# A scan with chunked steps in a hybrid inference kernel: outputs once per step, one diagonal for both heads' inverse, values token-major through DRAM, low-rank products in row halves

## The chip, the cores and the metric

One Trainium2 chip, and of it one core. The metric is device time in microseconds (us) of one execution. In profiles the engines are PE (TensorE's products), PEld (its weight loads), DVE (VectorE), ACT (ScalarE), POOL (GpSimd) and SP (SyncE, whose queue issues every DMA of this kernel, in order).

## What is computed

One step of a two-layer network on 1,024 latent tokens and 256 context tokens of width 1,024. Layer 0 is a dense projection, a bidirectional RWKV-7 scan over 8 heads of 64, a short convolution, and an output projection; layer 1 is attention. The change touches the scan of layer 0 only:

```python
def rwkv_scan(S0, r, w, k, v, kk, a, reverse):
    def step(S, inp):
        r_t, w_t, k_t, v_t, kk_t, a_t = inp
        sk = jnp.einsum('bhvk,bhk->bhv', S, kk_t)
        S = (S * w_t[:, :, None, :] - sk[..., None] * (kk_t * a_t)[:, :, None, :]
             + v_t[..., None] * k_t[:, :, None, :])
        return S, jnp.einsum('bhvk,bhk->bhv', S, r_t)
...
    w_log = -jax.nn.softplus(-(w0 + jnp.einsum('bldr,drc->bldc', jnp.tanh(lw), lw2))) - 0.5
    decay = jnp.exp(-jnp.exp(w_log.astype(f32)))
    a = jax.nn.sigmoid(a0 + jnp.einsum('bldr,drc->bldc', la, la2))
```

The scan runs forwards and backwards, both outputs are added, normalised per head, and gated.

## The kernel before

**The fill.** Layer 0's dense projection is 816 triples of products (`mm<-h_hi,whi`, `mm<-h_lo,whi`, `mm<-h_hi,wlo`: float32 split into two reduced-precision parts), 2,448 matmuls in `dense_g`. Its results are shifted and stored to DRAM in `rkv_d` (keys, normalised keys, r, v), `lora_d` and `sg_d` by the sinks of `s_part` and `a_part`.

**The scan.** Heads go in four pairs; a pair fills 128 partitions, 64 per head. A pair has five steps: four groups of 256 latent tokens, where step j does group j forwards and group 3-j backwards, and one step for the context. So there are 20 steps, each with two directions d and four chunks i of 64 tokens. A step goes through these generators:

- `load` and `prepare`: loads, the low-rank products `iv<-lor,lw` (both directions, 64 rows each, for decay and a), exponentials; makes `bk` and `s`.
- `interact`: products of keys with keys inside each chunk (`wk<-s,bk`), masked into `nn`, `br` and the other half of `s`; the transposes `wk<-ident,bk` that make `tbk`.
- `solve`: on DVE, the inverses of the 32x32 triangular diagonal blocks (`tmp`, `acc`: 62 small instructions), sent through DRAM (`w_d`) into the matrix `w`.
- `merge`: v is loaded (`vt`), transposed on PE (`iv<-ident,vt`) and copied into `hv`; then the off-diagonal block of the inverse: a transpose of one diagonal block by products with the identity (`iv<-ident,w`), a copy, products with `nn` (`iv<-t,nn`), a copy, products `iv<-w,zz`, a copy into `w`.
- `chain`: the recurrence over the four chunks, with the state in `hv`. Per chunk, in this order of dependence: `ch<-hv,s`, copy `xs`, `ch<-xs,w`, copy into `hv`, `ch<-hv,tbk`, four DVE instructions `hv<-ch,gc,hg` that write the next chunk's state. The outputs of the chunk are two groups of products, `py<-s,hv` and `py<-br,hv`, added into `y` per chunk and direction.
- `finish`: per-head normalisation (`iv<-y,ones`, `iv<-sqy,ones`), bonus, gate, store.

**What sets the order.** Each of these is a Python generator that says before each operation on which engine and for which tiles it waits. `Loom.run` is a planner with a clock per engine and a cost for each instruction: it takes the first generator in `PRECEDENCE` whose next operation could start soon enough, and issues it. So the program order on every engine is fixed when the kernel is built; on the chip, each engine runs its list in that order. The fill's generators stand low in the table, so dense triples go where no scan operation is ready. All recorded operations carry the line of one helper (L145), so the profile is read by tile names.

**Rings.** The PSUM banks are rings: `mm` 2, `wk` 2, `py` 2, `ch` 1, `iv` 1 banks. Two steps are under way at a time, by conditions such as this one, ahead of `solve`:

```python
            yield lambda: x.nr is not None and (x.n < 2 or steps[x.n - 2].done)
```

## Time and profile before

| | us |
|---|---|
| median of 3 runs (lowest to highest) | 2251.95 (2249.22 to 2253.41) |
| the profiled execution: its own time | 2253.86 |
| its span, first to last instruction | 2252.2 |
| layer 0's dense products and the scan beside them | from 64.9 to 1171.4 |
| attention layer and its projections | from there to the end |

The profiled execution is 1.9 us above the median. The last row of the scan is the product that turns the final context state round. Busy shares of the whole span are means over all stages; the stage of the scan has to be read by itself, with windows and the timeline. PE's matmuls are pipelined: the length of one overlaps the next, so the time that a group takes from PE is read from its start to the start of what follows it.

### The profile page before, as it was taken

What the parts mean: (1) busy time and instruction counts of PE and PEld (TensorE: products, weight loads), DVE (VectorE), ACT (ScalarE), POOL (GpSimd) and SP (SyncE); (2) the same over time, 40 slices, a digit from 0 to 9 for tenths busy, and PEclk for the clock granted to TensorE, in tenths of its full rate; (3) what the DMA queues carried; (4) which work ended last, traced back from release to release, by engine and by line L of the source; (5) the groups of instructions that cost most, each with busy time, mean ns of one, the idle gap of its engine ahead of it and who ended that gap; (6) DMA issues with size and microseconds to landing.
All of it is one profiled execution on the core that took longest, in us unless ns stands there. A gap on an engine that the chain in (4) does not pass through costs nothing.

```text
span 2252.2 us, 42921 instructions
## 1 busy us (share of the span) xinstructions
...
## 2 busy tenths in 40 slices
...
GB/s 271 305 98 131 98 105 131 85 68 114 102 97 103 99 96 101 85 111 54 86 153 185 206 111 88 99 87 107 82 53 48 60 42 38 43 28 71 58 131 108
DMA packets 337818, 232.86 MB, mean 103 GB/s; under 512 B 163890, under 2 KB 289860, under 8 KB 335556
## 3 DMA queue, kind: packets, MB, share of 16 engines
...
## 4 chain that ended last, share of the span: by engine, by line
PE 39%; DVE 9%; DMA 5%; issue 3%; ACT 1%; POOL 1%; SPq 1%; DVEq 0%; POOLq 0%; ACTq 0%
PE mm L145 21%; PE pv L145 8%; PE wk L145 5%; PE py L145 4%; DVE mx L145 3%; DVE rz L145 1%; DVE zs L145 1%; DMA rz<-rz_d 1%; PE ch L145 1%; DVE tmp L145 1%; SPq L145 1%; DVE acc L145 1%; DMA rz_d<-rc 1%; DMA rc<-rz 0%; DVE hv L145 0%
## 5 line engine op out<-in xcount | busy, mean ns | idle before, releaser
L145 POOL TENSOR_TENSOR zs<-zs,pe 128x512 f32<-128x512 f32 x275 | 366.8, 1370 | 34.1 <-ACT pe L145 32.1
L145 PE MATMUL mm<-h_hi,whi 128*128 128x512 f32 (+1 forms) x816 | 336.5, 412 | 4.3 <-ACT whi L145 4.1
L145 PE MATMUL mm<-h_hi,wlo 128*128 128x512 f32 (+1 forms) x816 | 299.3, 367 | 8.1 <-DVE wlo L145 7.2
L145 PE MATMUL mm<-h_lo,whi 128*128 128x512 f32 (+1 forms) x816 | 298.7, 366 | 0.0
L145 POOL TENSOR_TENSOR wlo<-wraw,whi 128x128 fp32r<-128x128 f32 x228 | 111.4, 494 | 246.0 <-ACT whi L145 205.8
L145 PE MATMUL pv<-pe,v_sb 128*64 128x512 f32 (+1 forms) x832 | 200.4, 604 | 0.0
L145 PEld LDWEIGHTS mm<-h_hi,whi 128*128 128x128 f32 x816 | 159.9, 196 | 49.5 <-issue 12.2
L145 PEld LDWEIGHTS mm<-h_hi,wlo 128*128 128x128 f32 x816 | 160.1, 196 | 37.1 <-DVE wlo L145 10.0
L145 DVE TENSOR_TENSOR acc<-acc,tmp 128x60 f32<-128x60 f32 (+23 forms) x620 | 168.0, 273 | 20.8 <-issue 2.9
L145 PE MATMUL mm<-wts,omh 128*128 128x512 f32 x648 | 166.6, 410 | 7.6 <-ACT wts L145 4.0
L145 PEld LDWEIGHTS mm<-h_lo,whi 128*128 128x128 f32 x816 | 161.0, 197 | 14.4
L145 PE MATMUL mm<-wts,h_hi 128*128 128x512 f32 x480 | 151.1, 396 | 0.0
L145 POOL TENSOR_TENSOR hg<-hv,gc 64x128 f32<-64x128 f32 x152 | 65.1, 428 | 185.0 <-DVE hv L145 173.9
L145 PEld LDWEIGHTS mm<-wts,omh 128*128 128x128 f32 x648 | 122.9, 194 | 38.0 <-ACT wts L145 5.3
L145 ACT ACTIVATE whi<-wraw 128x128 fp32r<-128x128 f32 x272 | 80.2, 305 | 78.2 <-DMA wraw<-in_w_in_e_dram 40.3
L145 DVE TENSOR_REDUCE mx<-mm 128x1 f32<-128x512 f32 (+1 forms) x138 | 89.7, 660 | 36.7 <-PE py L145 12.6
L145 DVE SCALAR_TENSOR_TENSOR hv<-ch,gc,hg 64x64 f32<-64x64 f32 x288 | 81.3, 282 | 49.3 <-PE ch L145 42.2
L145 POOL TENSOR_TENSOR xr<-xr,og 128x512 f32<-128x512 f32 x40 | 54.6, 1364 | 128.4 <-DVE og L145 93.3
L145 PEld LDWEIGHTS pv<-pe,v_sb 128*64 128x64 f32 x832 | 51.6, 139 | 93.9 <-issue 82.3
L145 DVE TENSOR_REDUCE mx<-py 128x1 f32<-128x512 f32 (+1 forms) x138 | 89.6, 660 | 28.7 <-PE mm L145 13.0
L145 DVE TENSOR_TENSOR tmp<-acc,nra 128x31 f32<-128x31 f32 (+7 forms) x320 | 90.1, 282 | 27.4 <-DMA acc<-eye_d 17.7
L145 ACT ACTIVATE pe<-py 128x512 f32<-128x512 f32 (+1 forms) x139 | 79.1, 587 | 60.3 <-PE mm L145 20.3
...
## 6 DMA issues: line engine op xcount, KB each, us to landing
...
```

Of the source, the lines that this page charges most:

```text
L145: r = f(*a, **k)
```

## The change

- **Outputs once per step.** `py` is one bank that holds both directions' 256 tokens. `chain` issues `py<-s,hv` right behind `ch<-hv,s`; a new generator `outputs` issues all `py<-br,hv` of a step at once when the four chunks are done, then one addition or copy into `y` per direction instead of one per chunk. The next chain takes the bank, so it waits for this.
- **Both heads' inverse on one diagonal.** `w` becomes 128 wide with each head's inverse in its own block, so `ch<-xs,w` is one 128-row product per direction instead of two 64-row ones. In `merge` the block's transpose is done by DVE (`STREAM_TRANSPOSE`) instead of PE and a copy; the off-diagonal block of `nn` comes from a copy in DRAM (`n12_d`, 2 stores and 2 loads per step), so `nn` needs one buffer.
- **v token-major through DRAM.** New generator `turn_v`: v is transposed right behind its dense product, forwards and backwards (PE 128x128 transposes, a reversing copy, a copy out of PSUM), and stored to `vt_d`; `values` loads `hv` from it with four DMAs per step. The transposes and copies in `merge` go. `bonus`, `merge` and `turn_v` share a ring of two tiles `t11`.
- **Low-rank products in row halves.** The two directions alternate, each into its own bank; `iv` has two banks, which also serve layer 0's first transposes in place of `py`.
- **A looser pipeline.** The conditions between steps are split: `solve` waits for its own step's inputs alone, the `tbk` transposes are a generator of their own, and flags `recurred` (the recurrence is over), `valued` and `done` (outputs too) take the place of `done`. `PRECEDENCE` has the new generators; the planner's cost for 64-row float32 products on more than 64 columns changes.

```diff
-        ((ps_mm, "mm", 2), (ps_wk, "wk", 2), (ps_py, "py", 2), (ps_ch, "ch", 1), (ps_iv, "iv", 1)))
+        ((ps_mm, "mm", 2), (ps_wk, "wk", 2), (ps_py, "py", 1), (ps_ch, "ch", 1), (ps_iv, "iv", 2)))
...
-    w_t = [rc.tile([P, 2, 4, C], F32, name=f"w{i}") for i in range(2)]
+    w_t = [rc.tile([P, 2, 4, P], F32, name=f"w{i}") for i in range(2)]
...
+    def s_v(p):
+        def sink(b, f, done):
+            t0, n, _ = BLK[b]
+            dma(out=sp[p][:, 3, t0:t0 + n], in_=f)
+            turns.append(turn_v(p, b, f, done))
+            yield lambda: True
...
+        t0, n, cd = BLK[b]
+        for z in range(2):
+            pt = None
+            for i in range(0, n, GRP):
+                x = f[:, i:i + GRP]
...
+                    back = f[:, n - i - GRP:n - i][:, ::-1]
...
+                for q in range(0, GRP, P):
+                    T.transpose(out=pt[:, i + q:i + q + P], in_=x[:, q:q + P], identity=ident)
...
+            r0 = t0 if z == 0 else NS + NT - t0 - n if cd else NS - t0 - n
+            dma(out=vt_d[p][z][r0:r0 + n].rearrange("(i q) v -> q i v", q=P),
+                in_=t[:, 0:n].rearrange("q (i v) -> q i v", v=P))
+            nbs.release(t)
...
-        for d in range(2):
-            yield "T", x.lor, lw2, iv_ps
-            pz = iv_ps.take()
-            for z in range(2):
-                T.matmul(pz[:, z * GRP:(z + 1) * GRP], lw2[HH[d], z, :], x.lor[HH[d], z, :], start=True, stop=True)
+        yield "T", x.lor, lw2, iv_ps, iv_ps
+        pzs = [iv_ps.take(), iv_ps.take()]
+        for z in range(2):
+            for d in range(2):
+                T.matmul(pzs[d][:, z * GRP:(z + 1) * GRP], lw2[HH[d], z, :], x.lor[HH[d], z, :], start=True, stop=True)
+        for d, pz in enumerate(pzs):
             for z in range(2):
...
+        for h in range(2):
+            dma(out=n12_d[x.n % 4][h], in_=x.nn.rearrange(CD)[64 * h:64 * h + 32, :, 32:64])
...
-        yield "T", w8, iv_ps
-        pa = iv_ps.take()
-        for i in range(8):
-            for h in range(2):
-                r1 = 64 * h
-                T.matmul(pa[r1:r1 + 32, i * 32:i * 32 + 32], w8[r1:r1 + 32, i, 0:32], ident[r1:r1 + 32, r1:r1 + 32],
-                         start=True, stop=True)
-        t11 = st1.tile([P, 256], F32, tag="t11", name="t11")
-        yield from copied(pa, *((t11[r:r + 32, :], pa[r:r + 32, 0:256]) for r in (0, 64)))
-        iv_ps.release(pa)
+        yield "V", w8, t11s[0]
+        t11 = t11s[0].take()
+        for rr in HH:
+            V.transpose(t11[rr].rearrange("p (i t) -> p i t", i=8), w8[rr, :, rr.start:rr.start + 32])
         yield "T", t11, iv_ps
         pa = iv_ps.take()
         for i in range(8):
             for h in range(2):
                 r1, r2 = 64 * h, 64 * h + 32
-                T.matmul(pa[r2:r2 + 32, i * 32:i * 32 + 32], bn8[r1:r1 + 32, i, 32:64], t11[r1:r1 + 32, i * 32:i * 32 + 32],
+                T.matmul(pa[r2:r2 + 32, i * 32:i * 32 + 32], x.n12[r1:r1 + 32, i, :], t11[r1:r1 + 32, i * 32:i * 32 + 32],
...
+    def values(x):
+        yield lambda: passed[f"t{x.p}"]
+        t0 = NS if x.j is None else x.j * GRP
+        for d in range(2):
+            for h in range(2):
+                dma(out=x.hv[HH[1 - h], h, d],
+                    in_=vt_d[x.p][d][t0:t0 + GRP, HH[h]].rearrange("(i t) v -> t i v", t=C))
...
+        py = x.py = py_ps.take()
         for i in range(4):
             c0 = i % 2 * 256
             pa, pu = (pc[:, c0 + q:c0 + q + 128].rearrange("p (d t) -> p d t", d=2) for q in (0, 128))
@@ -1161,13 +1216,14 @@
             for d in range(2):
                 for h, rr in enumerate(HH):
                     T.matmul(pa[rr, d], x.s[h][:, d, i, 0, :], x.hv[:, h, d, i, :], start=True, stop=True)
+            for d in range(2):
+                c1 = 256 * d + 64 * i
+                for h, rr in enumerate(HH):
+                    T.matmul(py[rr, c1:c1 + C], x.hv[:, h, d, i, :], x.s[h][:, d, i, 1, :], start=(d == 0 and i == 0),
+                             stop=False, skip_group_check=True)
             xs = chn.tile([P, 2, C], F32, tag="xs", name="xs", bufs=1)
             yield from copied(pa, (xs, pa))
-            yield "T", py_ps, py_ps
-            pys = [py_ps.take(), py_ps.take()]
-            for d in range(2):
-                for h, rr in enumerate(HH):
-                    T.matmul(pys[d][rr, 0:C], x.hv[:, h, d, i, :], x.s[h][:, d, i, 1, :], start=True, stop=False)
             if not last:
                 hg = chn.tile([P, 2, C], F32, tag="hg", name="hg", bufs=1)
                 for h, rr in enumerate(HH):
@@ -1176,8 +1232,7 @@
             yield "T", xs, x.w
             for d in range(2):
-                for rr in HH:
-                    T.matmul(pu[rr, d], x.w[rr, d, i, :], xs[rr, d], start=True, stop=True)
+                T.matmul(pu[:, d], x.w[:, d, i, :], xs[:, d], start=True, stop=True)
...
-            yield ("T",)
-            for d in range(2):
-                for h, rr in enumerate(HH):
-                    T.matmul(pys[d][rr, 0:C], x.hv[rr, h, d, i, :], x.br[rr, d, i, :], start=False, stop=True)
-            for d in range(2):
-                py = pys[d]
-                yield "V" if j is not None and j >= 2 else "S", py, 0.15
-                c0 = i * C if d == 0 else GRP - (i + 1) * C
-                ysl = y[d][:, c0:c0 + C]
-                if d == 1:
-                    ysl = ysl[:, ::-1]
-                if (j is not None and j >= 2) or c0 in seen:
-                    V.tensor_tensor(out=ysl, in0=py[:, 0:C], in1=ysl, op=ALU.add)
-                else:
-                    S.activation(ysl, py[:, 0:C], AF.Copy)
-                if j is None:
-                    seen.add(c0)
-                py_ps.release(py)
             if i < 3:
                 yield "T", x.hv[:, :, :, i + 1]
         ch_ps.release(pc)
         x.y = y
+    def outputs(x):
+        j, y, py = x.j, x.y, x.py
+        yield "T", x.hv, x.br
+        for d in range(2):
+            for i in range(4):
+                c1 = 256 * d + 64 * i
+                for h, rr in enumerate(HH):
+                    T.matmul(py[rr, c1:c1 + C], x.hv[rr, h, d, i, :], x.br[rr, d, i, :], start=False,
+                             stop=(d == 1 and i == 3), skip_group_check=True)
+        for d in range(2):
+            add = (j is not None and j >= 2) or (j is None and d == 1)
+            ysl = y[d] if d == 0 else y[d][:, ::-1]
+            yield "V" if add else "S", py, y[d], 0.3
+            if add:
+                V.tensor_tensor(out=ysl, in0=py[:, 256 * d:256 * d + 256], in1=ysl, op=ALU.add)
+            else:
+                S.activation(ysl, py[:, 256 * d:256 * d + 256], AF.Copy)
+        py_ps.release(py)
...
         for x in steps:
-            yield lambda: x.bk is not None and (x.n < 2 or steps[x.n - 2].inverted)
+            yield lambda: x.bk is not None and (x.n < 2 or steps[x.n - 2].solved) and (x.n < 3 or steps[x.n - 3].done)
             yield from interact(x)
+    def all_tbk():
+        for x in steps:
+            yield lambda: x.ready and (x.n < 2 or steps[x.n - 2].recurred)
+            yield from turn_keys_of(x)
     def all_solved(b):
         for x in steps[b::2]:
-            yield lambda: x.nr is not None and (x.n < 2 or steps[x.n - 2].done)
+            yield lambda: x.ready
             yield from solve(x)
     def all_merged():
         for x in steps:
-            yield lambda: x.ready and x.hv is not None
+            yield lambda: x.ready
             yield from merge(x)
             x.inverted = True
@@ -1444,9 +1514,21 @@
             for z in steps[x.n:x.n + 2] if x.n == 0 else steps[x.n + 1:x.n + 2]:
                 z.hv = chn.tile([P, 2, 2, 4, C], F32, tag="hv", name="hv")
-            yield lambda: x.inverted and x.prepared and (x.n < 2 or steps[x.n - 2].closed)
+            yield lambda: x.inverted and x.prepared and x.valued and (x.n < 2 or steps[x.n - 2].closed)
             yield from chain(x)
+            x.recurred = True
+    def all_put():
+        for x in steps:
+            yield lambda: x.recurred
+            yield from outputs(x)
             x.done = True
+    def all_valued():
+        for x in steps:
+            yield lambda: x.hv is not None and (x.n < 2 or steps[x.n - 2].done)
+            yield from values(x)
+            x.valued = True
```

The number of products on PE falls from 11,364 to 10,804 (one float32 product is two instructions in the trace), and the fill's 2,448 stay; SP's DMAs rise from 1,545 to 1,689. Three places show how the instructions lie.

PE, end of a step's chain (`ch` the chain's bank, `py` the outputs', `hv` the state, `omh` and `wts` the output projection's triples). Before, in the last step, from the third-but-last product of a chunk to the next chunk's first:

```order
L145 MATMUL ch_14288<-xs,w_195 64x64 x4
L145 MATMUL mm_14165<-wts_14353,omh_14232 128x512
L145 MATMUL mm_14165<-wts_14354,omh_14232 128x512
L145 MATMUL mm_14165<-wts_14353,omh_14233 128x512
L145 MATMUL ch_14288<-hv,tbk 64x64 x4
L145 MATMUL mm_14390<-wts_14373,omh_14144 128x512
L145 MATMUL mm_14390<-wts_14374,omh_14144 128x512
L145 MATMUL mm_14390<-wts_14373,omh_14145 128x512
L145 MATMUL py_14357<-br,hv 64x64 x2
L145 MATMUL py_14358<-br,hv 64x64 x2
L145 MATMUL ch_14288<-hv,s_12969 64x64
```

Now, the last chunk of the last step but one:

```order
L145 MATMUL ch_13377<-hv,s_12272 64x64
L145 MATMUL ch_13377<-hv,s_12273 64x64
L145 MATMUL ch_13377<-hv,s_12272 64x64
L145 MATMUL ch_13377<-hv,s_12273 64x64
L145 MATMUL py_13378<-s_12272,hv 64x64
L145 MATMUL py_13378<-s_12273,hv 64x64
L145 MATMUL py_13378<-s_12272,hv 64x64
L145 MATMUL py_13378<-s_12273,hv 64x64
L145 MATMUL ch_13377<-xs,w_194 128x64 x2
L145 MATMUL py_13378<-br,hv 64x64 x16
L145 MATMUL mm_13528<-wts_13557,omh_13266 128x512
L145 MATMUL mm_13528<-wts_13558,omh_13266 128x512
```

The output products with `s` stand behind `ch<-hv,s`, and those with `br`, of all four chunks, in one row of 16.

PE, the off-diagonal block of the inverse (`iv`) among the fill's triples. Before:

```order
L145 MATMUL iv_10590<-ident,w_195 32x32 x16
L145 MATMUL mm_10534<-h_hi,whi 128x512
L145 MATMUL mm_10534<-h_lo,whi 128x512
L145 MATMUL mm_10534<-h_hi,wlo 128x512
L145 MATMUL mm_10534<-h_hi,whi 128x512
L145 MATMUL mm_10534<-h_lo,whi 128x512
L145 MATMUL mm_10534<-h_hi,wlo 128x512
L145 MATMUL iv_10640<-t_10607,nn 32x32 x16
```

Now, on PE and then on DVE (where `nb` is a dense result that is being shifted, and `tmp`, `acc` are the solve of another step):

```order
L145 MATMUL iv_9935<-t_9926,n_9811 32x32 x16
L145 MATMUL mm_9956<-h_hi,whi 128x512
L145 MATMUL mm_9956<-h_lo,whi 128x512
L145 MATMUL mm_9956<-h_hi,wlo 128x512
L145 MATMUL mm_9956<-h_hi,whi 128x512
L145 MATMUL mm_9956<-h_lo,whi 128x512
L145 MATMUL mm_9956<-h_hi,wlo 128x512
L145 MATMUL iv_9968<-w_194,t_9926 32x32 x16
```

```order
L145 SCALAR_TENSOR_TENSOR nb_9896<-nb_9896,mm_9754 128x512
L145 STREAM_TRANSPOSE t_9926<-w_194 64x256 x2
L145 SCALAR_TENSOR_TENSOR nb_9952<-nb_9952,mm_9889 128x256
L145 STREAM_TRANSPOSE t_10002<-w_195 64x256 x2
L145 TENSOR_TENSOR tmp<-acc,nra 128x31
```

The 16 products with the identity are gone from PE, and two transposes stand on DVE.

PE, the low-rank products. Before, one direction, the other one standing 14 rows further on:

```order
L145 MATMUL mm_10687<-h_lo,whi 128x512
L145 MATMUL mm_10687<-h_hi,wlo 128x512
L145 MATMUL iv_10692<-lor,lw_10100 128x256 x2
L145 MATMUL mm_10687<-h_hi,whi 128x512
L145 MATMUL mm_10687<-h_lo,whi 128x512
L145 MATMUL mm_10687<-h_hi,wlo 128x512
```

Now both, alternating between the two banks:

```order
L145 MATMUL mm_10381<-h_hi,wlo 128x256
L145 MATMUL iv_10392<-lor,lw_9633 128x256
L145 MATMUL iv_10393<-lor,lw_9633 128x256
L145 MATMUL iv_10392<-lor,lw_9633 128x256
L145 MATMUL iv_10393<-lor,lw_9633 128x256
L145 MATMUL ch_10349<-hv,tbk 64x64 x4
```

All four stand together. Behind the last dense triple, PE's list holds the chain of one step before, and those of two steps now, with 54 products of the output projection among them up to the scan's last product before and 105 now.

## Rows read from the trace of the kernel before

**Rows 1.** Windows: length, busy us (count) by engine, granted clock, DMA share, GB/s.
```profile
270.00:1111.00 841.00, 754.27 (x8278) 555.66 (x8277) 665.11 (x1981) 464.59 (x1246) 326.80 (x551) 0.96 0.36 94
1111.00:1172.00 61.00, 43.61 (x360) 26.21 (x360) 35.01 (x87) 24.11 (x54) 15.14 (x18) 0.75 0.50 154
```

**Rows 2.** Tile view of the last third of a triple: min/median/max ns, first to last start.
```profile
L145 PE MATMUL mm<-h_hi,wlo x816: 274/389/796, 64.9 to 1110.7; 128*128 128x512 f32 x110, 128*128 128x256 f32 x54
```

**Rows 3.** Timeline of PE inside a step, 563 to 575 us: start, length, instruction.
```profile
563.50 1.13 PE L145 MATMUL iv<-lor,lw 64*128 64x256 f32 x4
564.56 0.45 PE L145 MATMUL ch<-hv,tbk 128*64 128x64 f32 x8
...
568.36 0.45 PE L145 MATMUL py<-s,hv 128*64 128x64 f32 x8
568.74 0.39 PE L145 MATMUL mm<-h_hi,whi 128*128 128x256 f32 x1
...
569.65 0.45 PE L145 MATMUL ch<-xs,w 64*64 64x64 f32 x8
570.02 0.39 PE L145 MATMUL mm<-h_hi,whi 128*128 128x256 f32 x1
...
572.99 0.45 PE L145 MATMUL py<-br,hv 64*64 64x64 f32 x8
573.37 0.66 PE L145 MATMUL wk<-ident,bk 128*128 128x128 f32 x4
573.95 0.69 PE L145 MATMUL iv<-ident,w 32*32 32x32 f32 x32
574.58 0.66 PE L145 MATMUL wk<-ident,bk 128*128 128x128 f32 x4
574.99 0.47 PE L145 MATMUL mm<-h_hi,whi 128*128 128x512 f32 x1
```

**Rows 4.** Timeline of PE behind the last dense product, 1147 to 1151 us.
```profile
1146.89 0.45 PE L145 MATMUL ch<-hv,s 128*64 128x64 f32 x8
1147.17 0.40 PE L145 MATMUL py<-s,hv 128*64 128x64 f32 x8
...
1148.20 0.99 PE L145 MATMUL mm<-wts,omh 128*128 128x512 f32 x3
...
1151.06 0.45 PE L145 MATMUL ch<-hv,s 128*64 128x64 f32 x8 [0.22 <-DVE hv L145]
```

**Rows 5.** Timeline of PE in the attention: products on two row halves.
```profile
1703.06 0.39 PE L145 MATMUL py<-qh,kh 64*128 64x512 f32 x2
1703.29 0.40 PE L145 MATMUL py<-qh,kl 64*128 64x512 f32 x2
```

**Rows 6.** Weight loads, 270 to 1111 us: busy us, mean ns, idle before.
```profile
L145 PEld LDWEIGHTS ch<-xs,w 64*64 64x64 f32 x600 | 24.2, 137 | 17.1 <-ACT xs L145 5.8 <-DVE xs L145 3.8 <-issue 1.4
...
L145 PEld LDWEIGHTS wk<-ident,bk 128*128 128x128 f32 x144 | 16.5, 140 | 8.2 <-DVE br L145 3.5 <-issue 1.2 <-ACT tbk L145 0.4
```

**Rows 7.** Waits of PE, 270 to 1111 us: us in total, times, longest.
```profile
PE ch L145 <- DVE hv L145: 18.5, 28, 2.8
...
PE iv L145 <- DMA w<-w_d: 1.9, 3, 1.1
```

**Rows 8.** Groups of DVE, 270 to 1170 us; the last, whole span.
```profile
L145 DVE TENSOR_TENSOR y<-py,y 128x64 f32<-128x64 f32 x80 | 14.3, 218 | 6.3 <-PE py L145 5.1
...
L145 DVE COPY hv<-iv 64x256 f32<-64x256 f32 x10 | 4.2, 418 | 0.2
...
L145 DVE STREAM_TRANSPOSE mt<-mx 128x32 f32<-128x32 f32 x24 | 5.0, 209 | 0.5
```

**Rows 9.** SP's queue, 270 to 1111 us: issue ns min/median/max; longest wait.
```profile
L145 SPq DMA_DIRECT2D w<-w_d x72: 547/600/1284, 278.8 to 1080.7; - x72
...
L145 SPq DMA_DIRECT2D vt<-rkv_d x18: 327/432/1175, 298.5 to 1090.3; - x18
...
SPq L145 <- POOL wlo L145: 107.1, 56, 10.6
```

178 lines of the change are left out of this document (107 added, 71 removed), and 4 rows, old and new, of the table PRECEDENCE.

## The prediction, made before the changed kernel ran

> **What bounds the kernel now.** I read the windows first, then the timeline of PE, then PE's waits, then the queue of SP. While the scan runs beside the dense products, PE is busy for 754.27 of 841 us at a granted clock of 0.96, that is near the upper of its two levels; DVE for 665.11, ACT for 464.59 [rows 1]. The dense triples fill every gap that the scan leaves on PE, and the last of them starts at 1110.7 [rows 2]. So in this stretch PE's work sets the end: what is taken off PE lets the last triple come earlier by as much, unless PE then waits more. Behind it 61 us follow in which PE is busy for only 43.61, at a clock of 0.75 [rows 1]: there the last steps' chains set the pace, one chunk in 1151.06 - 1146.89 = 4.17 us [rows 4]. Everything after the scan is unchanged in kind, so I take its time as fixed. PE's idle 87 us of the 841 is spread thin: the largest wait, for the state that DVE writes, is 18.5 us over 28 times [rows 7]. Therefore the sum is made in PE time, and each group costs what lies between its start and the start of the next group on the timeline, since the lengths themselves overlap.
>
> **The change part by part.** *Low-rank products in row halves.* One direction takes 564.56 - 563.50 = 1.06 us for four instructions [rows 3], and both, in 20 steps, 2 x 20 x 1.06 = 42. The attention shows what alternating row halves do: two 64-row products of 512 columns begin 0.23 us apart as a pair [rows 5]. That is 0.115 each, against 0.265 per 256 columns here, so halves that alternate do run side by side. Then all eight take about what four did, 1.06 us, and 20 x 1.06 = 21 us go. Bounds: 0 if these halves do not overlap, 21 if they do. I take 21, by the attention's row.
>
> *The transpose by identity.* `iv<-ident,w` takes 574.58 - 573.95 = 0.63 us [rows 3], once per step: 20 x 0.63 = 12.6 off PE, whole.
>
> *v transposed once.* Before, 40 groups of four transposes; a group of four like them takes 574.99 - 574.58 = 0.41 [rows 3], so 16.4 us. Now 80 single transposes in 29 bursts, 11 of four and 18 of two by the order: 11 x 0.41 + 18 x 0.20 = 8.1, or 29 x 0.41 = 11.9 if a burst costs the same whatever its size. Gain 4.5 to 8.3; I take 6.
>
> *Output products.* `py<-s,hv` alone is 568.74 - 568.36 = 0.38 [rows 3]; but right behind `ch<-hv,s`, the pair is cheaper, since the chain's own group then takes 1147.17 - 1146.89 = 0.28 rather than 0.38 [rows 4]: 0.10 x 80 chunks = 8 (0 if most stood so already). `py<-br,hv`, 573.37 - 572.99 = 0.38 four times per step, becomes one burst, 3 x 0.28 + 0.38 = 1.22 by the same difference: 0.30 x 20 = 6 (6 to 8). They also leave the middle of the chunk, which costs nothing while triples fill that place.
>
> *`ch<-xs,w`.* One 128-row product instead of two 64-row ones: 570.02 - 569.65 = 0.37 per chunk now [rows 3]. Two halves already ran side by side, so half as many products need not be quicker. The one thing that grows is the weight load, to 128 columns; a load of that width takes 140 ns here, one of 64 columns 137 [rows 6]. I take 0, with 3 us for a gain and 8 for a loss (80 x 0.10, the difference between the joined and the single group above).
>
> The sum on PE: 21 + 12.6 + 6 + 8 + 6 + 0 = 53.6, say **54 us**; with all the bounds on one side 15 (0 + 12.6 + 4.5 + 0 + 6 - 8), on the other 61 (21 + 12.6 + 8.3 + 8 + 8 + 3).
>
> *What is given back on DVE.* Two transposes of 64x256 per step are new. The nearest rows are 209 ns for 128x32 and 418 ns for a copy of 64x256 [rows 8]: 40 of them are 8 to 17 us. The additions into `y` shrink from 80 of 218 ns [rows 8], 17.4 us, to 20 of about 418: -9. Some 28 copies of `nn` stand on DVE that stood on ACT: 28 x 0.418 = +12. The copies into `hv`, 4.2 us [rows 8], go. In all +7 to +16, on top of 665, while the stretch gets 54 shorter: (665 + 12) / (841 - 54) = 86% instead of 79%. DVE does not become the bound, but PE will more often find the state unwritten. I charge half of the 18.5 us again: **+9**.
>
> *The end of the scan.* Two steps' chains stand behind the last triple now, one before: four more chunks at 4.17 us, 17 in all [rows 4]. With them 51 more products of the output projection are placed there, 17 triples of 0.99 us as in [rows 4], and these are taken off the time that follows. So 0 to 5, inside the 9.
>
> *SP's queue.* DMAs rise by 144: 40 stores and 40 loads for `n12`, 80 loads of `hv`, 24 stores of turned v, less 40 loads of `vt`. At 0.6 us per issue for the small pieces and 0.43 for the others [rows 9] that is 160 x 0.6 + 24 x 0.43 - 40 x 0.43 = 89 us more of issuing. Behind them in SP's order stand the loads of the dense weights. SP waits 107.1 us for a free raw weight tile [rows 9]; this slack pays for the 89, with 18 to spare. Cost 0, if the issues spread as the waits do; without this cover up to 89. The new waits inside SP's order, for `nn` before its store and for the state tile to be free before its load, hold up the weights queued behind in the same way.
>
> Forecast: 2253.9 - 54 + 9 = 2208.9 for an execution like the profiled one, which lay 1.9 above the median; so **2207**.
>
> **Rivals.** *DVE takes the gain back.* For it: 86% busy in order, the recurrence goes PE, ACT, DVE and round again, and steps now overlap more loosely, so a solve can stand in front of a state update. Against it: PE waits for DVE's state for only 18.5 us at 79%. If the wait doubles, and as much again falls on the inverse (the transpose and the copies of `nn` stand in the same queue), 2 x 18.5 = 37 returns: 2253.9 - 54 + 37 - 1.9 = 2235.
>
> *The change does not do on PE what it says.* If the low-rank halves do not run side by side, 21 are missing, and `ch<-xs,w` may lose its 8: the sum is 25, and less 9 that leaves 16, so 2236. For it: the attention's pair has another shape, 512 columns, and stands in another stage; against it the same row [rows 5].
>
> *SP's queue goes over its slack: slower.* SP issues in order, and `hv` for a step must be loaded before its chain. The price is the 89 us of issuing less what the 107.1 us of slack absorb. The slack is in 56 waits of at most 10.6 us [rows 9], while the new issues come in groups per step; each part that meets no wait holds up the next weights, and PE's triples with them. It decides from the point at which more than 45 of the 89 are exposed; at three quarters, 67: 2253.9 - 45 + 67 - 1.9 = 2274. For it: every triple needs the weights that stand behind these issues. Against it: 56 waits are nearly three per step, so most groups of issues meet one.
>
> *The small pieces arrive late.* `hv` now comes in pieces of 256 bytes and `n12` of 128, and the chain and the merge wait for them. `w<-w_d`, which also comes in pieces of 128, made PE wait 1.9 us in all, 1.1 at most [rows 7]; if every step pays that longest wait, 20 x 1.1 = 22 us come back: 2229. Against it: the row's total is a tenth of that. By the Trainium skill, "DMA: Bandwidth & Descriptors", Specifications, a transfer needs pieces of 512 bytes for full rate, so it expects such loads to be slow.
>
> *The wide weight loads show in full, and loss and gain cancel.* `ch<-xs,w` has 320 loads in the changed kernel, now twice as wide. If each took 137 ns [rows 6] more and none of it were hidden, 44 us come back: 2253.9 - 54 + 9 + 44 - 1.9 = 2251. Against it: 140 against 137 ns for the two widths. By the Trainium skill, "TensorE: Matmul & The Clock Gate", section on LDWEIGHTS, the time of a load goes with its number of columns; these two rows do not agree with that.
>
> **How the numbers follow.** Forecast 0.58; DVE 0.12; PE's sum missed 0.06; late pieces 0.04; cancelled 0.06; slower 0.14. A measurement of this kernel can tell about 0.2% (4.5 us) from no change; hence faster 0.58 + 0.12 + 0.06 + 0.04 = 0.80, same 0.06, slower 0.14. The range goes below to a sum of 61 with nothing given back and the 18.5 us of waits gone through the looser order, 2253.9 - 61 - 18.5 - 1.9 = 2172; above to 2250, which takes in the three rivals that are faster and leaves the two others out, 0.20.
>
> **What the profile after would show.** Right: a low-rank group of eight instructions in about 1.06 us; `py<-s,hv` 0.28 behind `ch<-hv,s`; one group of `py<-br,hv` per step at about 1.2; no `iv<-ident,w` and `iv<-ident,vt`; the last triple near 1111 - 45 = 1066, not 1110.7, and the scan's last product some 40 to 50 us ahead of 1171. PE's busy time before it lower by about 50 with the idle time a little higher; SP's wait for the raw tile far below 107. Wrong: PE idle much more than 87 us, with DVE's `hv` or the inverse named; PE waiting for `wlo`, `whi` or a DMA of `hv`; a low-rank group of 2 us; `ch<-xs,w` far above 0.37.

## The result and the profile after

The changed kernel takes 2280.74 us (median of 4 runs, 2274.15 to 2283.3) against 2250.82 for the kernel before in the same comparison: a ratio of 1.0127, 95% interval 1.0103 to 1.0152. It is slower, where 2207 and a range up to 2250 were forecast. Its profiled execution spans 2277.9 us.

Windows of the changed kernel, with the columns of [rows 1]:

```profile
270.00:1111.00 841.00, 719.74 (x7194) 553.22 (x7194) 657.82 (x1917) 403.93 (x1045) 328.13 (x551) 0.91 0.40 101
1111.00:1207.00 96.00, 71.60 (x575) 51.27 (x575) 58.36 (x167) 34.35 (x78) 24.62 (x31) 0.77 0.44 129
```

Against [rows 1], PE is busy for 719.74 of the 841 us and not 754.27, so the work did go; but the end did not come nearer. The granted clock is 0.91 and not 0.96, and behind 1111 there are 96 us of scan and not 61. The tile views (lengths min/median/max, first to last start) tell the same at the two marks of the prediction. The last third of a triple:

```profile
L145 PE MATMUL mm<-h_hi,wlo x816: 274/389/795, 65.0 to 1117.8; 128*128 128x512 f32 x110, 128*128 128x256 f32 x54
```

And the product that ends the scan:

```profile
L145 PE MATMUL iv<-ident,h x32: 218/242/268, 534.4 to 1207.0; 64*64 64x64 f32 x32
```

The last triple starts at 1117.8, not at the forecast 1066 and even 7 us behind the 1110.7 of [rows 2]; the last product at 1207.0, where it was 1171.4. The rest of the program, from there to the end of the span, takes 1071 us instead of 1081. So the whole loss, and more, lies in the scan: 36 us more up to its last product, 10 less behind it, where fewer products of the output projection are left (105 of them stand ahead of that mark now, 54 before).

Where in the scan? The tile view of each chunk's first product, `ch<-hv,s`, in the kernel before:

```profile
L145 PE MATMUL ch<-hv,s x640: 222/222/370, 272.9 to 1157.1; 128*64 128x64 f32 x160
```

and in the changed one:

```profile
L145 PE MATMUL ch<-hv,s x640: 221/222/370, 308.5 to 1192.3; 128*64 128x64 f32 x160
```

From the first to the last of these it is 884.2 us before and 883.8 now. On the mean the twenty steps go at the same pace; the first one begins 36 us later and the end is 36 us later. A kernel whose end was set by PE's work would have got a faster pace from less of it. (Under other tables, further down, the same loss lies in the pace.)

The prices of the prediction, though, can be found on PE's timeline of the changed kernel, at full clock (start, length, instruction; a group costs what lies between its start and the next):

```profile
897.39 1.14 PE L145 MATMUL iv<-lor,lw 64*128 64x256 f32 x8
898.46 0.45 PE L145 MATMUL ch<-hv,tbk 128*64 128x64 f32 x8
```

and at the end of a chain:

```profile
1100.07 0.45 PE L145 MATMUL ch<-hv,s 128*64 128x64 f32 x8
1100.35 0.40 PE L145 MATMUL py<-s,hv 128*64 128x64 f32 x8
1100.69 0.50 PE L145 MATMUL mm<-h_hi,whi 128*128 128x512 f32 x1
...
1101.48 0.55 PE L145 MATMUL ch<-xs,w 128*128 128x64 f32 x4
1101.84 0.47 PE L145 MATMUL mm<-h_hi,whi 128*128 128x512 f32 x1
...
1104.68 1.15 PE L145 MATMUL py<-br,hv 64*64 64x64 f32 x32
1105.76 0.66 PE L145 MATMUL wk<-ident,bk 128*128 128x128 f32 x4
```

All eight low-rank instructions take 1.07 us, where four took 1.06 [rows 3]; `ch<-hv,s` 0.28 and `py<-s,hv` behind it 0.34; the step's one burst of `py<-br,hv` 1.08 (1.22 was assumed); `ch<-xs,w` 0.36 here, where a triple follows, against 0.37. What PE waits for, in 270 to 1111 us (total, times, longest):

```profile
PE ch L145 <- DVE hv L145: 19.1, 23, 3.0
...
PE iv L145 <- DMA n<-n_d: 8.9, 3, 8.4
...
PE mm L145 <- DVE wlo L145: 6.9, 2, 5.4
```

`hv` costs what it did in [rows 7]; new is the wait for the inverse. The product for its off-diagonal block, before and now, in the same window (count, busy us, mean ns, then the idle time of PE just before it):

```profile
L145 PE MATMUL iv<-t,nn 32*32 32x32 f32 x576 | 12.5, 192 | 1.0 <-ACT t L145 1.0
```

```profile
L145 PE MATMUL iv<-t,n 32*32 32x32 f32 x576 | 15.5, 200 | 22.1 <-DVE tmp L145 9.5 <-DMA n<-n_d 8.9 <-DVE t L145 3.1
```

PE idles for 22.1 us ahead of it instead of 1.0, for DVE and for the loads of the block, `n<-n_d`, one of them 8.4 us. In all PE idles for 121 us of the 841, where it was 87: that is one of the prediction's signs of being wrong. And SP's wait for a free raw weight tile, the slack of the rival with the queue:

```profile
SPq L145 <- POOL wlo L145: 99.1, 70, 9.5
```

It is 99.1 against 107.1 [rows 9]: the 144 new issues took hardly any of it.

### The profile page after: what moved, and what is told of

Read it like the earlier page. It is cut to its first block, busy times and chain, and to the rows that moved or that the text cites. A ratio compares the mean times of both kernels' runs of the same rounds, so it can differ in the third digit from the quotient of the medians.

```text
span 2277.9 us, 40969 instructions
## 1 busy us (share of the span) xinstructions
PE 2025.0 (89%) x14266; PEld 1415.8 (62%) x14266; DVE 1483.5 (65%) x3487; ACT 998.7 (44%) x2288; POOL 1022.3 (45%) x1158
## 4 chain that ended last, share of the span: by engine, by line
PE 45%; DVE 17%; DMA 7%; issue 4%; SPq 3%; ACT 2%; POOL 1%; DVEq 0%; POOLq 0%; ACTq 0%
PE mm L145 24%; PE pv L145 9%; PE wk L145 5%; SPq L145 3%; DVE mx L145 3%; PE py L145 2%; DVE tmp L145 2%; DVE acc L145 2%; PE ch L145 2%; DVE rz L145 2%; DVE hv L145 1%; PE iv L145 1%; DMA n_d<-nn 1%; DVE zs L145 1%; DMA rz<-rz_d 1%
## 5 line engine op out<-in xcount | busy, mean ns | idle before, releaser
L145 PE MATMUL mm<-h_hi,whi 128*128 128x512 f32 (+1 forms) x816 | 341.5, 418 | 17.8 <-DVE nb L145 9.1
L145 PE MATMUL mm<-h_hi,wlo 128*128 128x512 f32 (+1 forms) x816 | 307.0, 376 | 16.7 <-DVE wlo L145 14.6
L145 PE MATMUL mm<-h_lo,whi 128*128 128x512 f32 (+1 forms) x816 | 304.8, 373 | 0.0
L145 DVE TENSOR_TENSOR acc<-acc,tmp 128x48 f32<-128x48 f32 (+22 forms) x620 | 166.1, 274 | 17.8 <-issue 2.3
L145 PEld LDWEIGHTS mm<-h_lo,whi 128*128 128x128 f32 x816 | 165.8, 203 | 15.3
L145 POOL TENSOR_TENSOR hg<-hv,gc 64x128 f32<-64x128 f32 x152 | 70.0, 460 | 229.7 <-DVE hv L145 223.1
L145 DVE TENSOR_REDUCE mx<-pv 128x1 f32<-128x512 f32 (+1 forms) x139 | 90.4, 661 | 33.1 <-PE mm L145 17.1
L145 DVE TENSOR_TENSOR tmp<-acc,nra 128x31 f32<-128x31 f32 (+9 forms) x320 | 88.4, 277 | 36.0 <-DMA acc<-eye_d 28.0
L145 ACT ACTIVATE pe<-mm 128x512 f32<-128x512 f32 (+1 forms) x140 | 79.7, 584 | 66.4 <-PE pv L145 22.1
L145 PE MATMUL mm<-h_hi,wts 128*128 128x512 f32 (+1 forms) x384 | 104.9, 358 | 0.0
```

Of the source, the lines that this page charges most:

```text
L145: r = f(*a, **k)
```

## Experiments

Two kinds of run were made. In the first, a kernel keeps the order of every engine word for word, and only some instructions are left out of the lists, so nothing but their work is missing. In the second the code or the table is changed and the planner makes its order anew.

### Less work on PE, in the same order

```diff
             T.matmul(pt[:, 0:n], hi, xh, start=(k == 0), stop=False)
-            T.matmul(pt[:, 0:n], hi, xl, start=False, stop=False)
             T.matmul(pt[:, 0:n], lo, xh, start=False, stop=(k == KT - 1))
```

The planner still counts the product, so the order stays; it is not issued.

Expected of before_thin:

> The kernel before, every engine's order as it was, but the middle product of each dense triple (h_lo with whi, 816 of 2,448) is left out, so its output lacks that part. By 0.23 us for 512 columns (544) and 0.12 for 256 (272) this takes 158 us of work off PE. Theory 'PE's work sets the end' (the base of the prediction): about 2251 - 158 = 2093, at least 110 faster. Rival 'the steps of the scan set the end, and the dense products only fill PE': not below 2200, since the chain of steps keeps its 20 periods of 45.6 us.

Expected of after_thin:

> The changed kernel, same order, with the same 816 products left out. If PE's work sets its end: about 2281 - 158 = 2123. If the steps' own chain does (interact, a DMA round trip, solve on DVE, another round trip, merge, chain): not below 2240. If the kernel before gains over 110 and this one much less, the change itself moved the bound from PE to the steps.

Measured: before_thin 2253.41 us, ratio to the kernel before 0.9998 (0.9973 to 1.0023). after_thin 2275.21, ratio 1.0091 (1.0061 to 1.0120), where the changed kernel has 1.0127. **Taking 816 products, 158 us at full clock, off PE is worth nothing before, and after some 8 us by the ratios, with intervals that overlap.** A window of before_thin (columns as in [rows 1]):

```profile
65.00:1111.00 1046.00, 869.57 (x8487) 608.79 (x8486) 769.37 (x2185) 566.93 (x1481) 405.76 (x667) 0.85 0.39 106
```

and its tile views of the last third of a triple,

```profile
L146 PE MATMUL mm<-h_hi,wlo x816: 274/393/797, 65.2 to 1117.6; 128*128 128x512 f32 x110, 128*128 128x256 f32 x54
```

and of the scan's last product:

```profile
L146 PE MATMUL iv<-ident,h x32: 218/267/366, 495.0 to 1177.2; 64*64 64x64 f32 x32
```

The last triple is not 158 us earlier but at 1117.6. (That is 7 later than in [rows 2], which means nothing: this profiled execution took 2266.12 us, 13 above its median.) PE is busy for 869.57 us of these 1046, by the same view 943.46 in the kernel before: 74 less, not 158, because the granted clock is 0.85 instead of 0.96, so what is left runs slower; and it idles for 74 us more. The chain's own products are among those that run slower (`ch<-hv,s` 259 ns on the mean from 270 to 1111 us, 243 before), so a small gain of the scan may have been cancelled by the clock; no run separates the two. The largest waits from 65 to 1171 us (total, times, longest):

```profile
PE wk L146 <- ACT sq L146: 32.2, 18, 6.3
PE ch L146 <- DVE hv L146: 21.1, 26, 3.4
PE mm L146 <- DVE wlo L146: 15.4, 7, 4.2
```

What does set the pace can be read off the same run, where PE is no suspect any more. Timeline of PE from the last chunk of step 12 to the first of step 14:

```profile
843.67 0.45 PE L146 MATMUL ch<-hv,s 128*64 128x64 f32 x8
...
893.13 0.69 PE L146 MATMUL iv<-ident,w 32*32 32x32 f32 x32
...
898.60 0.69 PE L146 MATMUL iv<-w,zz 32*32 32x32 f32 x32
...
900.94 0.45 PE L146 MATMUL ch<-hv,s 128*64 128x64 f32 x8
```

and of DVE, the first and one of the last instructions of the solve of step 14:

```profile
856.46 0.19 DVE L146 TENSOR_TENSOR tmp<-acc,nra 128x31 f32<-128x31 f32 x1 [4.41 <-DMA acc<-eye_d]
...
884.37 0.17 DVE L146 TENSOR_TENSOR tmp<-acc,nrb 128x8 f32<-128x8 f32 x1
```

A solve may start when the step two before it is done. Step 12's last chunk begins at 843.67; the start value `acc` of step 14's solve must still come from DRAM, and the solve begins at 856.46, after a wait for that load. It goes on to 884, then its result goes through DRAM, at 893.13 to 898.60 the merge runs, and at 900.94 the chain of step 14 begins. When that is over, step 16 may be solved. This is a loop over two steps that goes through DVE, SP's DMAs, ACT and PE, and in the kernel before its mean turn is 91 us: 884.2 us from the first chunk to the last, less some 17 for the last chain, over 19 steps, twice. The triples lie in its gaps. The timelines of PE and DVE of the kernel before have it in every step: a solve begins 0.8 to 16.3 us behind the last output product of two steps before.

The changed kernel has another loop. Its solves begin up to 50 us ahead of that product, but the first product of `interact` in a step stands 0 to 28 us behind the last output product of three steps before, 10 on the mean, as its new condition says. One turn takes three steps and 137 us, so the pace per step, 45.5 us, is what it was (45.6). What the looser order should have won is lost inside the turn: a solve takes 45 us on the mean, 38 before, and from its end to the first instruction of its merge 18 us go by, 11 before. In step 15, the widest gap between two chains, the inverse is loaded and then waits for its transposes behind the whole solve of step 16. From SP's queue and DVE's timeline of the changed kernel:

```profile
982.62 2.55 SPq L145 DMA_DIRECT2D w<-w_d  x4
...
1025.92 0.18 DVE L145 TENSOR_TENSOR acc<-acc,tmp 128x8 f32<-128x8 f32 x1
...
1027.04 0.90 DVE L145 STREAM_TRANSPOSE t<-w 64x256 f32<-64x256 f32 x2
```

The first line issues the loads of step 15's inverse, the second is the last instruction of step 16's solve, the third the transposes of step 15. Under the new table that is tried below, the 18 us are 9.7, as in the kernel before under its own new table, and the loss remains; so this is what one order did, not what the change costs in every order.

### Less work on DVE, in the same order

```diff
-        for t in range(31):
+        for t in range(16):
             m, n = t // 4 + 1, 31 - t
```

(The planner again counts all 31.)

Expected of before_solve_half:

> The kernel before, same order, but the later half of each solve is left out: 30 of its 62 small DVE instructions per step (those that read nrb), 600 in all, so its output is another one. In the trace of before a solve begins 5 to 20 us after the end of the chain two steps earlier, at every step; the loop is chain, loads for the solve, solve (38 us), round trip of w, merge, chain, 91 us per two steps. Theory 'this loop sets the end': a solve gets some 16 to 19 us shorter, 10 loops, so 100 to 160 us faster until PE bounds, 2090 to 2150. Rival 'PE or SP sets the end': within 20 us of before.

Expected of after_solve_half:

> The changed kernel, same order, with the same 600 DVE instructions of the solves left out. Theory 'the loop through DVE's solve sets the end here too, now over three steps (137 us)': 80 to 140 us faster than the changed kernel, 2140 to 2200. Rival 'SP's queue sets it': less than 30 us faster, 2250 or more.

Measured: 2209.85, ratio 0.9805 (0.9774 to 0.9837), and 2246.79, ratio 0.9971 (0.9949 to 0.9992). So 600 small instructions on DVE are worth 44 us before and some 35 us after, where 816 large ones on PE were worth next to none: the solve is on the path. But both gains lie between the two theories' ranges, far under the 100 and 80 us that a path of solves alone should have given. A window of before_solve_half,

```profile
65.00:1111.00 1046.00, 960.96 (x9670) 702.71 (x9666) 663.94 (x1683) 589.78 (x1530) 422.48 (x684) 0.96 0.41 114
```

and its tile view of the scan's last product:

```profile
L146 PE MATMUL iv<-ident,h x32: 218/242/268, 484.9 to 1121.8; 64*64 64x64 f32 x32
```

DVE is down by 113 us (777.31 in the same window before), the scan ends 50 us earlier, and PE is busier, 960.96 us against 943.46. That PE's work stands next once the loop is 50 us shorter fits these rows; it was not tested by a run that lightens both.

### The parts that go through DRAM, for free, in the same order

In after_free_n12 the n12 tile is constant, in after_free_v the value halves of `hv` are. The diffs show what is left out; in the second the transposes, the copies and the stores of `turn_v` go, and the order stays:

```diff
-        for h in range(2):
-            dma(out=n12_d[x.n % 4][h], in_=x.nn.rearrange(CD)[64 * h:64 * h + 32, :, 32:64])
...
-            dma(out=x.n12[64 * h:64 * h + 32], in_=n12_d[x.n % 4][h])
```

```diff
-                dma(out=x.hv[HH[1 - h], h, d],
-                    in_=vt_d[x.p][d][t0:t0 + GRP, HH[h]].rearrange("(i t) v -> t i v", t=C))
...
-            turns.append(turn_v(p, b, f, done))
```

Expected of after_free_n12:

> The changed kernel, same order, but the 40 stores of nn's off-diagonal block to DRAM and the 40 loads of n12 are left out (n12 is a constant tile, so the output is another one). Theory 'SP's in-order queue is what costs': 80 issues of about 0.52 us (42 us of SP) and PE's 14.7 us of waits for these loads go, with the low clock behind them: 20 to 35 us faster, about 2250. Rival 'the new DVE transposes in merge, which stand behind the solves, cost': less than 10 us, 2270 or more.

Expected of after_free_v:

> The changed kernel, same order, but with the values for free: turn_v's 80 transposes, 40 or so copies and 24 stores and the 80 loads of hv are left out (hv's value halves stay constant, so the output is another one). Theory 'SP's in-order queue': 104 DMAs less, 45 us of SP, and DVE's 15 us of waits for the nb buffers: 20 to 40 us faster. Rival 'the off-diagonal block and the merge are what costs': only the 8 to 12 us that the transposes take on PE, 2268 or more.

Measured: after_free_n12 2276.56, ratio 1.0092 (1.0068 to 1.0116), an interval that overlaps that of the changed kernel: 80 DMAs less and the waits for `n<-n_d` are worth 4 us by the medians, 8 by the ratios. The off-diagonal block's way through SP's queue is not the main cause. after_free_v 2260.50, ratio 1.0026 (1.0004 to 1.0048): 20 us less by the medians, 23 by the ratios. Tile view of the chunks' first products in after_free_v,

```profile
L146 PE MATMUL ch<-hv,s x640: 222/222/369, 304.1 to 1173.6; 128*64 128x64 f32 x160
```

and of the scan's last product:

```profile
L146 PE MATMUL iv<-ident,h x32: 218/242/267, 528.5 to 1188.2; 64*64 64x64 f32 x32
```

The first chunk comes 4 us earlier than in the changed kernel, the last product 19: turning v costs in all stages, not only in the start. It is no net price, since the kernel before also has to turn v. Nor does the run say which part costs: 104 DMAs, 80 transposes and their copies go together.

### One part alone: the looser solve

```diff
-            yield lambda: x.nr is not None and (x.n < 2 or steps[x.n - 2].done)
+            yield lambda: x.nr is not None
...
+        yield lambda: x.n < 2 or steps[x.n - 2].done
         x.solved = True
```

Expected of before_loose:

> The kernel before with one condition of the change alone: a solve waits only for its own inputs, no longer for the step two before it to be done (only its result then waits for that). The order is planned anew. Theory 'the loop is a dependence': the solve leaves the loop, which gets shorter by the 12 us of loads and part of the solve: at least 40 us faster, 2210. Theory 'DVE is shared': the solve of a third step now stands ahead of the chain's state updates on DVE, each piece takes longer and nothing is won: 2240 to 2275.

Measured: 2286.18, ratio 1.0132 (1.0084 to 1.0180): this one condition, in the kernel before, loses as much as the whole change. The tile view of the chunks' first products:

```profile
L145 PE MATMUL ch<-hv,s x640: 221/222/370, 265.9 to 1184.1; 128*64 128x64 f32 x160
```

Its first chunk is 7 us earlier than before, its last 27 later: 918 us instead of 884. But the edit did not do on the chip what it was meant to. The last output products of step 12 and the first instruction of step 14's solve:

```profile
864.36 0.45 PE L145 MATMUL py<-br,hv 64*64 64x64 f32 x8
```

```profile
871.75 0.59 DVE L145 TENSOR_TENSOR tmp<-acc,nra 128x31 f32<-128x31 f32 x1 [1.87 <-DMA acc<-eye_d]
```

In every step the solve still begins behind the outputs of two steps before, by 0.2 to 19.3 us, 8.6 on the mean, where it was 7.5. It had no earlier input: the `interact` that feeds it still waits for the merge two steps back. So neither theory was tested, no solve of a third step stands beside the chain's state updates, and what the run measures is another order.

### Orders of like quality

That run has another order, too, so how much is an order worth? For each of the next kernels the table `PRECEDENCE` was searched anew: 350 to 400 random steps, each exchanging neighbours or changing a lead number, and the planner's own estimate decided which table stayed. The last two columns of this table and of the next come from one profiled execution each, up to 14 us off its kernel's median. Such a table differs in many small places, as here in the changed kernel's:

```diff
-              ("chained", 0), ("prepared", 0.2), ("valued", 0), ("put", 0),
+              ("chained", 0), ("valued", 0.1), ("put", 0),
...
-              ("interacted", 0), ("tbk", 0), ("solved1", 0), ("solved", 0), ("finished", 0.1), ("merged", 0),
+              ("interacted", 0.2), ("h1", 1.0), ("tbk", 0), ("solved1", 0), ("solved", 0), ("finished", 0.1),
+              ("prepared", 0), ("merged", 0.3),
```

Expected of after_retable:

> The changed kernel with nothing but another PRECEDENCE: 'prepared' back behind 'finished', and then a table found in 400 random steps (two neighbours exchanged, one lead number changed) that the planner ranks first. Theory 'the order is what the change lost by, its parts are worth something': at least 35 us faster than the changed kernel and faster than before, 2240 or less. Rival 'a part (values through DRAM, the merge on DVE, SP's queue) costs whatever the order': 2265 or more.

Expected of before_retable:

> Control: the kernel before with another PRECEDENCE from a search of the same size. If its own table was as good as can be found: 2245 to 2260. If an order alone is worth tens of us for either kernel: 2235 or less, and the gain of the changed kernel under its new table has to be read against this one.

before_rows_retable, the kernel before with this edit:

```diff
-        for d in range(2):
-            yield "T", x.lor, lw2, iv_ps
-            pz = iv_ps.take()
+        rings = [iv_ps, wk_ps]
+        yield "T", x.lor, lw2, iv_ps, wk_ps
+        pzs = [q.take() for q in rings]
+        for z in range(2):
+            for d in range(2):
```

Expected of before_rows_retable:

> The kernel before with one part of the change alone, the low-rank products in row halves (the second bank borrowed from wk), and a table from a search of the same size. Prediction's price: 21 us of PE, group of eight in 1.06 us. Theory 'PE's work sets the end': 21 us below the control. Theory 'the steps set the end': within 10 us of the control, whatever the group takes.

Expected of before_loose_retable:

> The kernel before with the looser solve alone (as before_loose) and a table from a search of the same size. If the looser condition itself costs (solves of a third step stand ahead of the chain's state updates on DVE): 10 to 30 us above the control. If before_loose lost only by a bad draw of the order: within 8 us of the control.

| kernel, table of its own | median us | ratio to before (95%) | last triple | scan's last product |
|---|---|---|---|---|
| before_retable | 2220.57 | 0.9827 (0.9792 to 0.9862) | 1093.0 | 1160.4 |
| before_rows_retable | 2224.87 | 0.9836 (0.9795 to 0.9878) | 1078.4 | 1148.7 |
| before_loose_retable | 2231.32 | 0.9877 (0.9837 to 0.9916) | 1098.1 | 1173.1 |
| after_retable | 2253.09 | 0.9981 (0.9953 to 1.0008) | 1053.6 | 1201.2 |

An order alone is worth 1.7% to the kernel before and 1.4% to the changed one. **before_retable is the fastest of the kernels that compute all**, with no other edit than its table, and it beats both. Part of that gain lies behind the scan, since the table orders the attention too: from the scan's last product to the end of the span it is 1081 us before, 1063 in before_retable and 1047 in after_retable. But the gap between the two kernels stays, 1.3% under their own tables and 1.5% under the new ones, so, as far as these few tables tell, a bad order alone is not what the change lost by. Where it loses has changed, though. The chunks' first products in before_retable,

```profile
L185 PE MATMUL ch<-hv,s x640: 222/222/369, 269.2 to 1146.3; 128*64 128x64 f32 x160
```

and in after_retable:

```profile
L189 PE MATMUL ch<-hv,s x640: 222/222/369, 273.9 to 1186.6; 128*64 128x64 f32 x160
```

The late start is gone, all but 5 us, and the steps now go slower: 912.7 us from the first to the last, against 877.1.

The looser solve, which cost 31 us under the old table, costs 11 under its own, with intervals that overlap. The row halves bring nothing in the time: the last triple is 15 us earlier and the scan's last product 12, but the rest of the program, which the table orders too, takes 15 longer. (This kernel also has the changed planner's cost for 64-row products.) The tile view of the last third of a triple in after_retable,

```profile
L189 PE MATMUL mm<-h_hi,wlo x816: 274/389/796, 67.9 to 1053.6; 128*128 128x512 f32 x110, 128*128 128x256 f32 x54
```

of its scan's last product,

```profile
L189 PE MATMUL iv<-ident,h x32: 216/218/268, 505.3 to 1201.2; 64*64 64x64 f32 x32
```

a window between the two,

```profile
1050.00:1165.00 115.00, 67.36 (x713) 48.45 (x708) 90.45 (x270) 36.10 (x93) 35.71 (x50) 0.67 0.39 99
```

and what PE waits for, from 65 to 1171 us:

```profile
PE ch L189 <- DVE hv L189: 30.6, 29, 3.3
PE mm L189 <- DVE wlo L189: 23.2, 14, 3.4
...
PE iv L189 <- DVE t L189: 14.3, 9, 9.8
```

The last triple starts at 1053.6, 57 us earlier than in [rows 2], near the 54 of the sum on PE; but 18 of them the kernel before also got from a new table (1093.0), so 39 are left for the change. The scan's last product stands at 1201.2, where the changed kernel had 1207.0. What was gained on PE became the window behind the last triple, in which PE is busy for 67.36 of 115 us at a clock of 0.67. The last row, 1.4 us in before_retable, is nearly new with the change: PE waits for DVE's transposes in the merge.

### One part undone, each with its own table

undo_values, in which v is loaded per step, transposed on PE and copied again:

```diff
-                dma(out=x.hv[HH[1 - h], h, d],
-                    in_=vt_d[x.p][d][t0:t0 + GRP, HH[h]].rearrange("(i t) v -> t i v", t=C))
+            dma(out=v, in_=sp[x.p][:, 3, x.tok[d]:x.tok[d] + GRP])
...
+                T.transpose(out=pv[0:64, i * P:(i + 1) * P], in_=v[:, i * C:(i + 1) * C], identity=ident)
...
+            yield from copied(pv, (x.hv[64:128, 0, d], pv4[0:64, :, 0, :]))
```

Expected of undo_values:

> The changed kernel, undone in one part: v is again loaded per step, transposed on PE and copied into hv (turn_v and its loads go); its own table from 400 random steps, as after_retable (2253). Theory 'values through DRAM cost' (20 us came when they were left out): 2228 to 2240. Rival 'the merge on DVE costs': 2248 or more.

undo_merge, in which the block's transpose is on PE again:

```diff
-        yield "V", w8, t11s[0]
...
-            V.transpose(t11[rr].rearrange("p (i t) -> p i t", i=8), w8[rr, :, rr.start:rr.start + 32])
+        yield "T", w8, iv_ps
...
+                T.matmul(pa[r1:r1 + 32, i * 32:i * 32 + 32], w8[r1:r1 + 32, i, r1:r1 + 32], ident[r1:r1 + 32, r1:r1 + 32],
```

Expected of undo_merge:

> The changed kernel, undone in one part: the transpose of the diagonal block is again 16 products with the identity on PE and copies, not two transposes on DVE; own table. Under its own table the changed kernel's PE waits 14.3 us for these transposes (DVE t), 9.8 at the longest. Theory 'the merge on DVE costs, since it stands among the solves': 2228 to 2242. Theory 'PE's work counts': 12 us slower, 2265. Rival 'values': 2248 to 2258.

undo_loose, in which a solve waits for the recurrence of the step two before it:

```diff
         for x in steps[b::2]:
-            yield lambda: x.ready
+            yield lambda: x.ready and (x.n < 2 or steps[x.n - 2].recurred)
```

Expected of undo_loose:

> The changed kernel, undone in one part: a solve waits again for the end of the recurrence two steps before it; own table. In the kernel before the looser solve cost 31 us under the old table and 11 under its own. Theory 'the looser pipeline costs': 2235 to 2245. Rival 'it only hurts where the order is bad': 2248 to 2258.

undo_outputs, in which the outputs are finished in each chunk:

```diff
+            yield "T", py_ps
+            py = py_ps.take()
...
+                    T.matmul(py[rr, 256 * d:256 * d + C], x.hv[rr, h, d, i, :], x.br[rr, d, i, :], start=False,
...
+            py_ps.release(py)
```

Expected of undo_outputs:

> The changed kernel, undone in one part: the products with br and the additions into y again per chunk, the outputs' bank taken and freed per chunk; own table. Theory 'the one bank of the outputs, held over a whole step, delays the next chain': 2235 to 2245. Rival 'outputs once per step are harmless or a gain': 2253 or more.

The last three runs put the last two edits together, with two tables, and give the changed kernel a second table:

Expected of undo_both_a:

> The changed kernel with two parts undone, the looser solve and the outputs per step; own table from a search of 350 steps. Theory 'these two are the loss, the parts on PE are gains': both add up, 2215 to 2235, at or under the kernel before with its own new table (2221). Rival 'the differences of 10 us are draws of the table': 2240 to 2260.

Expected of undo_both_b:

> The same kernel with the best table of another search, which the planner ranks within 0.1% of the first. If tables of like rank run alike: within 5 us of undo_both_a. If the draw is worth as much as the parts: 10 us or more apart.

Expected of after_retable_b:

> The changed kernel with the best table of another search of 400 steps, begun from the table of the change itself, which the planner ranks 1.5% behind that of after_retable. If an order is worth tens of us: 2255 to 2285. If the loss of the changed kernel were one bad draw: 2240 or less.

| kernel | median us | ratio to before (95%) | last triple | scan's last product |
|---|---|---|---|---|
| undo_values | 2267.08 | 1.0030 (1.0013 to 1.0048) | 1117.4 | 1218.1 |
| undo_merge | 2273.69 | 1.0066 (1.0043 to 1.0089) | 1152.9 | 1226.5 |
| undo_loose | 2245.40 | 0.9937 (0.9905 to 0.9969) | 1086.5 | 1192.8 |
| undo_outputs | 2249.16 | 0.9936 (0.9910 to 0.9961) | 1102.5 | 1185.9 |
| undo_both_a | 2251.72 | 0.9963 (0.9941 to 0.9986) | 1091.3 | 1188.2 |
| undo_both_b | 2261.53 | 1.0014 (0.9992 to 1.0037) | 1109.6 | 1194.2 |
| after_retable_b | 2263.60 | 1.0018 (0.9996 to 1.0041) | 1131.5 | 1201.2 |

No part gives back the 1.5% when it is undone alone. Undoing the values or the merge's transpose makes it slower by 0.5 and 0.9%, undoing the looser solve or the outputs faster by 0.45%; undoing both of these is not faster still. Two tables of like rank for the same kernel lie 0.5% apart (undo_both_a and undo_both_b); after_retable and after_retable_b, which the planner ranks 1.5% apart, differ by 0.4%. So differences of 10 us between single tables are draws, and of these four runs only undo_merge stands somewhat clear of that, on the side that the part is a gain. What is clear is the two families: three kernels built on the code before lie at 0.983 to 0.988, the changed code with two tables of its own at 0.998 and 1.002, and five kernels with a part or two undone at 0.994 to 1.007.

## Why the prediction was wrong

**The base: "PE's work sets the end".** This is the step that failed. It was read from PE busy for 90% of a stretch, and from triples in every gap. before_thin shows that 158 us less of that work changes nothing: the triples fill gaps of a loop that goes through DVE, DMAs, ACT and PE, 91 us for two steps, and whose last product is the end. The rows for a better reading were at hand: the 61 us behind the last triple in which PE is 43.61 busy [rows 1], and the last step's products in [rows 4], say that when the triples are out the scan is still under way; if its steps keep their pace, a triple that ends sooner only lengthens that tail. A busy share says how full an engine is, not that its work is late; for that the dependent work has to be followed over one turn of the loop, from the end of a chain to the solve two steps on.

**The terms of the sum on PE.** Nearly all right as prices, and none of it came back as time. Low-rank halves: 1.07 for eight at full clock, 21 us off, and before_rows_retable is not faster than its control. `ch<-hv,s` 0.28 with `py<-s,hv` behind it, as assumed, and that itself 0.34 (1100.69 - 1100.35), where it was 0.38; `py<-br,hv` 1.08, cheaper than 1.22. The transposes of v were worth more than the 6 taken: 23.6 us of busy PE from 270 to 1111 us before (`iv<-ident,vt`), 11.7 now (`wk<-ident,t` and `wk<-ident,nb`). The term that was mis-sized is `ch<-xs,w`. Its 0.36 against 0.37 holds in 35 of the 80 groups, all with a triple behind them; in the 12 that stand in front of `wk<-s,bk` it takes 0.48 to 0.59, where the kernel before had 0.28. All its products on PE, before and now, 270 to 1111 us (count, busy us, mean ns, idle before):

```profile
L145 PE MATMUL ch<-xs,w 64*64 64x64 f32 x600 | 34.6, 235 | 8.7 <-DVE w L145 3.8 <-DVE xs L145 3.4 <-ACT xs L145 1.4
```

```profile
L145 PE MATMUL ch<-xs,w 128*128 128x64 f32 x288 | 45.2, 283 | 2.7 <-ACT e L145 2.1 <-ACT xs L145 0.2
```

That is 11 us more, part of it at the lower clock, beyond the 8 that were given as its bound for a loss, while 0 was taken. Nor were its weight loads as short as the prediction took them to be. Weight loads of the changed kernel (busy us, mean ns, idle before):

```profile
L145 PEld LDWEIGHTS ch<-xs,w 128*128 128x128 f32 x288 | 43.8, 203 | 10.1 <-ACT xs L145 2.7 <-ACT e L145 2.3 <-issue 1.0
...
L145 PEld LDWEIGHTS wk<-ident,bk 128*128 128x128 f32 x144 | 17.2, 150 | 5.5 <-PE wk L145 1.8 <-issue 0.6 <-PE py L145 0.5
```

203 ns, against 137 for the 64-column form [rows 6]; the clock, 0.91 against 0.96, may account for a small part of that (`wk<-ident,bk` went from 140 to 150). By the Trainium skill, "TensorE: Matmul & The Clock Gate", section on LDWEIGHTS, a load's time goes with its columns: this row leans that way, with half as much again rather than double. Load lengths of another kind of product, the 140 of `wk<-ident,bk`, were no guide. Where a triple follows, the group still takes 0.36, so the longer loads are hidden there; whether they make the 0.48 to 0.59 elsewhere, no run separates.

**DVE's added work.** Sized about right. The groups of DVE (count, busy us, mean ns, idle before):

```profile
L145 DVE STREAM_TRANSPOSE t<-w 64x256 f32<-64x256 f32 x40 | 17.4, 435 | 8.9 <-DMA w<-w_d 8.4
...
L145 DVE COPY nn<-wk 32x256 f32<-32x256 f32 x17 | 7.0, 414 | 6.9 <-PE mm L145 5.4 <-PE wk L145 1.1 <-ACT nn L145 0.3
...
L145 DVE TENSOR_TENSOR y<-py,y 128x256 f32<-128x256 f32 x17 | 6.5, 415 | 1.0 <-PE py L145 0.7
```

The 40 transposes cost 17.4 us, at the upper of the two bounds; additions and copies of `nn` cost 415 and 414 ns each, as assumed. (The 17.4 us of the old additions are count times mean; they overlap, and [rows 8] has them busy for 14.3.) The rival "DVE takes the gain back" was put as a matter of its share, 86%. The share is 657.82 of 841, 78%, no higher than the 79% before [rows 1]. What counts is where DVE's instructions stand in the loop: halving the solve gave 44 us. The other half of that rival, as much again in waits for the inverse, did come: 22.1 us of idle PE ahead of `iv<-t,n`, 12.6 of them for DVE, where 18.5 were named.

**The end of the scan.** 0 to 5 us were given; the scan's last product came 36 us later, 10 of which the rest gave back. This was the second error: the tail was priced as a few chunks more, while its start, and with it all twenty steps, had moved.

**SP's queue, the rival that had the right sign and size** (2274), is not what the runs point to: the slack is still there (99.1), after_free_n12 with 80 DMAs less has nearly the time of the changed kernel, and undo_values with 64 less is slower than after_retable. That the time came near 2274 is luck. Late small pieces there were, 8.9 us of PE's waits with one of 8.4, and without them and their DMAs the time is 4 to 8 us less. By the Trainium skill, "DMA: Bandwidth & Descriptors", Specifications, a transfer needs pieces of at least 512 bytes for full rate; whether their size or their place in the queue made these late, no run here separates.

**A looser pipeline** was counted as an edit that costs nothing, or saves waits (the lower end of the range). In the changed kernel's trace it won no pace: the turn of two steps became one of three. What the condition alone costs is not shown. In the kernel before it moved no solve, and its 31 us under the old table, 11 under its own, go with the order.

**What stays open.** Why the changed code is slower at all, with or without its own order: which part, or which pair, makes it 1.5% slower than the code before under tables of an equal search. By these runs it is not the order alone, not n12's DMAs, not the looser solve or the outputs alone, nor these two together. What all undone kernels still share and no run here separates: one buffer for `nn` and n12, `interact` waiting for the outputs of three steps back (in after_retable it begins 33 us behind them on the mean, so there this wait is not tight), the `tbk` transposes as a generator of their own, and the banks (two for `iv`, one for `py`). The same-order runs hold an order that was made for full triples; whether a new order would use a lighter PE better was not tried.
